# A hybrid encoder layer on one core: its last phase replanned and rearranged, with an earlier table load, one split on another engine and a third room for attention loads

## The chip, the cores and the metric

The kernel runs on one core of a Trainium2 chip. The engines of a core work side by side, each through its own queue in order, and wait for each other by semaphores: PE (TensorE) multiplies matrices, DVE (VectorE), ACT (ScalarE) and POOL (GpSimd) work on tiles, SP (SyncE) issues transfers; POOL issues some transfers as well. The metric is the device time of one execution in microseconds (us), the median of several; lower is better.

## The reference, cut to what matters

One layer is applied to 1536 tokens (a sequence of 1024 and one of 512) of width 1024, in fp32, with a feed-forward width of 2816:

```
h   = rmsnorm(x);  q, k, v, rec_x, rec_gate, g_attn, g_rec = split(h @ w_in)
A   = local_attention(rope(q), rope(k), v, sink)          # |i - j| <= 128
R   = bidir_rglru(centred_conv(rec_x)) * gelu(rec_gate)
merged = sigmoid(g_attn) * (A @ w_attn_proj) + sigmoid(g_rec) * (R @ w_rec_proj)
x   = x + rmsnorm(merged @ w_out)
h   = rmsnorm(x)
f   = (silu(h @ w_gate) * (h @ w_up)) @ w_ffn_out
y   = x + rmsnorm(f)
```

## The kernel before, in words

Tokens lie along the free axis, in three chunks of 512; 0 and 1 are the long sequence, 2 is the short one. Features lie on the 128 partitions, so a tile is 128 x 512 and a width of 1024 is eight tiles. fp32 accuracy is made out of three faster products: every operand is split into a high part (a copy by ACT into a shorter format, `hi`, or the first line of `split`) and a low part (operand less high part, on DVE or POOL, `lo`), and the products high-high, high-low and low-high are summed in PSUM (lines 353 to 355 before the last phase, 1377 to 1379 in it). A weight or operand is thus ready only when two engines have worked on it.

The start computes the first norm's factors in two halves of 256 tokens: squares by ACT, their sum over partitions by a product with ones, `Abs_reciprocal_sqrt` by ACT and three steps by DVE (`rstd_from`). ACT evaluates functions from tables, and another set of functions must first be loaded (ACT_TABLE_LOAD). Then come the projections v, k, q. `Stream` brings their weights: SP loads, ACT makes the high part, and the engine in the list `specs` the low one; entries `w_z[ZQ + j]` are the query weights. A rotary embedding of each query tile (lines 479 to 482) is done by DVE.

The middle does the RG-LRU and the attention with gate products between attention blocks. `att_load` brings a block's v, k and four q tiles through the rooms `braw`, of which there are two; a load waits until the room's last user has read it. The same SP queue carries the weight loads of `Stream` (line 318).

The last phase begins at the planner `Sched`. Each step is an `Op` on engine E (PE), V, P, A or S (SP's transfers), or Q (a transfer issued by POOL, used where it adds to what is in memory, `accum_op`), and "VP" lets it choose DVE or POOL. The planner simulates the phase with estimated times and writes each step into its engine's queue in the order in which it would start; on the chip the queues then run in that fixed order. PE's order of products is written out in a list `SEQ`: chunk 2 plainly ("B"), chunks 0 and 1 with a scheme of seven products for eight ("A"), stage by stage: attention and recurrent projections (pa, pr), out-projection (wo), FFN in (fi), FFN out (fo). Weights run through three raw rooms (`rw`) and six rooms for split ones (`sw`), gate tiles through two rooms (`ld`).

After the out-projection comes `first_norm`, for chunk 2 with 8 tiles and for chunks 0 and 1 with 16: each mix tile is loaded, multiplied by the norm's factor, and the layer's input x is added to it by a transfer that POOL issues and that accumulates into the tile (`added`). `second` squares the tile into room `a`, adds it to a sum, and stores the tile to yT. `rstd` then multiplies the sum by ones on PE (line 1195) and makes the next norm's factor; every FFN operand waits for that.

The last entries of `SEQ` are two halves of chunk 2's FFN out (`b_fo`), each 22 operand tiles (`bo`, loaded from `fsp` and split) times four PSUM banks. `b_tail` squares and copies each bank, the final `rstd` follows, and eight `last_out` multiply a tile by the factor and add it to yT by accumulating transfers.

Of the kernel before, what the change touches and what calls it, by code (L numbers as in the profile page):

```python
# [18 lines left out]
KD = 8  # L19
T = 1536  # L20
CH = 512
# [104 lines left out]
class Sched:  # L126
# [45 lines left out]
    def run(self):  # L172
        while self.programs:
# [14 lines left out]
            if eng in "SQ":  # L188
                self.t[queue] = at + (0.4 if eng == "S" else 0.7)
                self.wire = max(self.wire, at + 1.3) + op.n * 512 / 300e3  # L190
                end = self.wire + 0.7
            else:
                end = self.t[eng] = self.end(op, eng, at)
                if eng == "P":
                    self.port = end
# [8 lines left out]
def layer(ctx, tc, xT, par, w_z, w_v, w_g, w_pa, w_prA, w_prB, w_o, w_fi, w_foA, w_foB, rope, cst, yT):  # L204
# [24 lines left out]
    eps_t = const.tile([128, 1], F32, name="eps_t")  # L229
    dve.memset(eps_t, EPS)  # L230


# [137 lines left out]
    specs = [(w_v[j], wpair, dve) for j in range(2)] + [(w_z[ZK], wpair, dve), (w_z[ZK + 1], bpair, dve)]  # L370
    specs += [(w_z[ZQ + j], wpair, pool) for j in range(NQ)]
    for n in range(NL):
# [345 lines left out]
    def att_load(kv, c):  # L718
# [4 lines left out]
        def load(nm, src):  # L723
            r = b1.tile([128, 640], F32, name=f"{nm}{kv}{c}", tag="braw", bufs=2)
            n = src.shape[1] * (src.shape[2] if len(src.shape) > 2 else 1)
            sp.dma_start(r[:, :n] if len(src.shape) == 2 else r[:, :n].rearrange("p (b d) -> p b d", d=128), src)
            return r[:, :n]
# [458 lines left out]

    def rstd(a):

        done = []
        S.spawn(rstd_steps(a, done), -1)  # L1190
        yield lambda: done

    def rstd_steps(a, done):
        ps = yield from PS.take()
        yield Op("E", 4 * CH, lambda e: e.matmul(ps.t, ones, a.t, start=True, stop=True), [a], [ps])
        t = yield from HB.take()
# [25 lines left out]
    def first_norm(todo, xroom, aroom, c0, sums, queue):  # L1222

        xq, aq = [], []

        def no(x, k, n):
            yield from ()

# [8 lines left out]
        for _ in todo:  # L1237
            a, k, n = yield from get(aq)
            b = (yield from get(xq))[0]
            c, s = c0 + n, sums[n]  # L1240
            yield from tt(b.t, b.t, r[n].t, ALU.mult, [b, r[n]], [b], "VP")
            yield from added(None, xT[k * 128:(k + 1) * 128, c * CH:(c + 1) * CH], b)
            S.spawn(second(k, c, n, a, b, s, n in seen), 3)
            seen.add(n)
            queue.append(b)
# [252 lines left out]
    ROOM = [4 * i + 3 for i in range(PROD)] + [0, 1, 2, 4, 5, 6, 8, 9, 10, 12, 13, 14, 16, 17, 18, 20, 21]  # L1498
    tail, fin = {}, {}

# [7 lines left out]
    def b_fo(half):  # L1508
# [3 lines left out]
        if half == 0:  # L1512
            acc["f", 2] = yield from NM.take()
        for k in range(KF):
            s = yield from get(SQ)
# [4 lines left out]
            x.free, x.stage = True, None  # L1520
            SR.put(s)
        for i in range(4):
            m = 4 * half + i
            S.spawn(scaled("f", O_NFPOST, fof, m, 2, banks[i], True) if half == 0 else b_tail(m, banks[i]), 1)

    def b_tail(m, bank):
        o = fin[m, 2] = yield from roomy(40 + m)
        yield from square_add(("f", 2), bank, bank.t)
        yield from actv(o.t, bank.t, AF.Copy, [bank], [o], scale=P_[:, O_NFPOST + m:O_NFPOST + m + 1])
        PS.put(bank)  # L1530
# [30 lines left out]
    def build_b():  # L1561
# [14 lines left out]
        for m in range(4):  # L1576
            fin[m, 2] = yield from roomy(40 + m)
            yield from load(fin[m, 2], fof[m, 2])
        yield lambda: n_acc.get(("f", 2)) == KD
        r = acc["f", 2]  # L1580
        yield from rstd(r)
        for m in (4, 5, 6, 7, 0, 1, 2, 3):
            yield from last_out(m, 2, fin[m, 2], r)

    def start_rest():
# [101 lines left out]
```

## Time and profile before

| what | value |
|---|---|
| runs | 2469.33, 2470.05, 2472.5 us; median 2470.05 |
| profiled execution | 2475.74 us, of which the span 2474.0 |
| mean granted clock of PE | 0.991 |
| busy in the span | PE 97%, PE weight load 81%, DVE 68%, ACT 47%, POOL 31% |
| products of the last phase, lines 1377 to 1379 | the first six lines of the chain that ended last, from 17% down |

The span is the stretch that the trace covers. PE is busy nearly throughout, so an edit off PE counts only where PE waits for it, and in the serial stretch at the end.

### The profile page before, as it was taken

How to read it: one execution, taken by the hardware profiler on the slowest of the kernel's cores; microseconds unless marked ns; L12 is line 12 of the kernel's file. 1: busy time of each engine (PE TensorE's matmuls, PEld its weight loads, DVE VectorE, ACT ScalarE, POOL GpSimd, SP SyncE). 2: the span in 40 equal slices, each digit the busy share in tenths (PEclk: the TensorE clock that was granted, in tenths of full speed). 3: DMA queues.
4: the chain of work that ended last, by engine and by line, in shares of the span. 5: the costliest groups of instructions: out<-in, count | busy, mean ns of one | idle time of the engine just before them, and what ended most of it. 6: DMA issues, size and time to landing. Idle time of an engine off the chain costs nothing.

```text
span 2474.0 us, 30302 instructions
## 1 busy us (share of the span) xinstructions
PE 2409.9 (97%) x10878; PEld 1994.2 (81%) x10878; DVE 1688.5 (68%) x2454; ACT 1165.2 (47%) x1947; POOL 768.9 (31%) x602
## 2 busy tenths in 40 slices
PE   7999999999999999999999999999999999999996
PEld 5888888888878788888877888788888888888875
DVE  7864368686767665357867767875555568688794
ACT  5211567676645555444553445533333344344652
POOL 2322132424311122114334323143333333244242
PEclk9999999999999999999999999999999999999998
DMA  5222011111233332467686629422222234457557
GB/s 180 68 94 73 26 47 56 49 54 55 87 127 96 96 107 88 160 221 200 237 235 144 196 98 265 170 93 77 78 94 85 77 121 145 161 157 187 185 172 171
DMA packets 133063, 311.40 MB, mean 126 GB/s; under 512 B 14992, under 2 KB 23312, under 8 KB 132880
## 3 DMA queue, kind: packets, MB, share of 16 engines
q1 hardware_dynamic: 108880, 250.21, 30.6%
q0 software_dynamic: 22304, 57.68, 9.6%
q8 instruction: 85, 1.39, 0.2%
q10 hardware_dynamic: 1728, 1.57, 0.2%
q14 instruction: 66, 0.54, 0.1%
HBM read 215.03 MB, written 94.37 MB: 125 GB/s over the span
## 4 chain that ended last, share of the span: by engine, by line
PE 85%; issue 4%; DVE 3%; DMA 3%; POOL 2%; ACT 2%; SPq 0%; POOLq 0%; ACTq 0%; DVEq 0%
PE bk L1379 17%; PE bk L1377 17%; PE bk L1378 17%; PE pgt L354 3%; PE pgt L353 3%; PE pgt L355 3%; PE prg L354 2%; PE prx L354 2%; PE prg L355 2%; PE prx L355 2%; PE prg L353 2%; PE prx L353 2%; PE psq L355 2%; PE psq L354 2%; PE psq L353 2%
## 5 line engine op out<-in xcount | busy, mean ns | idle before, releaser
L1379 PE MATMUL bk<-ao,sw 128*128 128x512 f32 x1370 | 535.0, 390 | 2.3 <-DVE sw L964 2.3
L1377 PE MATMUL bk<-ao,sw 128*128 128x512 f32 x1370 | 536.3, 391 | 0.0
L1378 PE MATMUL bk<-ao,sw 128*128 128x512 f32 x1370 | 534.8, 390 | 0.0
L964 DVE TENSOR_TENSOR sw<-rw,sw 128x512 fp32r<-128x512 f32 (+2 forms) x358 | 313.7, 880 | 108.3 <-ACT sw L961 108.1
L964 DVE TENSOR_TENSOR co<-co,bk 128x512 f32<-128x512 f32 x326 | 218.9, 683 | 176.5 <-PE bk L1379 173.8
L961 ACT ACTIVATE sw<-rw 128x512 fp32r<-128x512 f32 (+2 forms) x381 | 228.1, 607 | 211.9 <-PE bk L1378 151.9
L1379 PEld LDWEIGHTS bk<-ao,sw 128*128 128x128 f32 x1370 | 258.1, 188 | 56.4 <-DVE sw L964 2.8
L1378 PEld LDWEIGHTS bk<-ao,sw 128*128 128x128 f32 x1370 | 258.3, 189 | 54.3 <-issue 0.8
L1377 PEld LDWEIGHTS bk<-ao,sw 128*128 128x128 f32 x1370 | 258.2, 188 | 54.2 <-issue 0.8
L1377 PE MATMUL bk<-bo,sw 128*128 128x512 f32 x656 | 258.8, 395 | 0.0
L1378 PE MATMUL bk<-bo,sw 128*128 128x512 f32 x656 | 255.9, 390 | 0.2 <-DVE bo L964 0.2
L1379 PE MATMUL bk<-bo,sw 128*128 128x512 f32 x656 | 255.8, 390 | 0.0
L961 ACT ACTIVATE sw<-tw 128x512 fp32r<-128x512 f32 (+2 forms) x138 | 81.8, 601 | 202.7 <-PE bk L1378 145.8
L304 POOL TENSOR_TENSOR w<-wr,w 128x1024 fp32r<-128x1024 f32 (+2 forms) x56 | 122.4, 2194 | 152.2 <-ACT w L303 151.8
L961 ACT ACTIVATE ao<-ta 128x512 fp32r<-128x512 f32 x166 | 101.3, 626 | 123.7 <-DVE ta L964 91.9
L353 PE MATMUL pgt<-h,w 128*128 128x512 f32 x384 | 156.4, 407 | 0.0
L354 PE MATMUL pgt<-h,w 128*128 128x512 f32 x384 | 151.4, 394 | 0.0
L355 PE MATMUL pgt<-h,w 128*128 128x512 f32 x384 | 151.2, 394 | 0.0
L622 DVE TENSOR_TENSOR i<-i,xc 128x1536 f32<-128x1536 f32 x20 | 71.1, 3589 | 113.0 <-ACT i L620 113.0
L1378 PEld LDWEIGHTS bk<-bo,sw 128*128 128x128 f32 x656 | 123.5, 188 | 27.7 <-issue 1.7
L1377 PEld LDWEIGHTS bk<-bo,sw 128*128 128x128 f32 x656 | 123.5, 188 | 27.1 <-issue 1.7
L1379 PEld LDWEIGHTS bk<-bo,sw 128*128 128x128 f32 x656 | 123.4, 188 | 25.5
(279 smaller groups left out, 4861.9 us busy)
## 6 DMA issues: line engine op xcount, KB each, us to landing
rw<-w_fi SPq DMA_DIRECT2D x88, 512.0 KB, 3.6
wr<-w_z SPq DMA_DIRECT2D x46, 512.0 KB, 3.7
ld<-gsp SPq DMA_DIRECT2D x48, 256.0 KB, 3.5
fsp<-co SPq DMA_DIRECT2D x44, 256.0 KB, 2.3
ta<-fsp SPq DMA_DIRECT2D x44, 256.0 KB, 3.9
bo<-fsp SPq DMA_DIRECT2D x44, 256.0 KB, 4.5
rw<-w_foB SPq DMA_DIRECT2D x22, 512.0 KB, 4.1
gsp<-gst POOLq DMA_DIRECT2D x42, 256.0 KB, 2.3
```

The source lines that it names most:

```text
L304: eng.tensor_tensor(out=lo, in0=x, in1=f32(hi), op=ALU.subtract)
L353: pe.matmul(ps, wh, xh, start=start and k == 0, stop=False)
L354: pe.matmul(ps, wh, xl, start=False, stop=False)
L355: pe.matmul(ps, wl, xh, start=False, stop=stop and k == n - 1)
L622: dve.tensor_tensor(out=I[d], in0=I[d], in1=xc, op=ALU.mult)
L961: yield Op("A", n, lambda e: e.activation(out, in_, func, **kw), R, W)
L964: yield Op(eng, n, lambda e: e.tensor_tensor(out=out, in0=a, in1=b, op=op), R, W)
L1377: pe.matmul(bank, wh, xh, start=first, stop=False)
L1378: pe.matmul(bank, wh, xl, start=False, stop=False)
L1379: pe.matmul(bank, wl, xh, start=False, stop=last)
```

## The change

There are eight edits in it. The planner now takes a POOL transfer to end 5.0 us after the wire is done with it, not 0.7, which reorders the queues of the last phase. ACT runs one activation of `Abs_reciprocal_sqrt` at the very start. The first query weight's low part goes to DVE. `braw` has three rooms. In `first_norm` the last three eighths of the tiles (three of chunk 2, six of chunks 0 and 1) get x by a load of SP into room `a` and an addition on DVE or POOL, in place of the accumulating transfer. In `b_fo(1)` the last four operand tiles are multiplied bank after bank, and each bank's `b_tail` starts when it is done. The eighth square is not added to the sum by DVE; a second product with ones adds it in PSUM (`rstd`'s `more`). At the end tiles 3 to 7 of yT are loaded early, and a multiplication and an addition on DVE and a plain store replace the accumulating transfer; tiles 0 to 2 keep it, and the order is 0 to 7.

```diff
@@ -188,7 +188,7 @@
             if eng in "SQ":
                 self.t[queue] = at + (0.4 if eng == "S" else 0.7)
                 self.wire = max(self.wire, at + 1.3) + op.n * 512 / 300e3
-                end = self.wire + 0.7
+                end = self.wire + (0.7 if eng == "S" else 5.0)
             else:
                 end = self.t[eng] = self.end(op, eng, at)
                 if eng == "P":
@@ -228,6 +228,7 @@
     negc, halfc = lru[:, 0, :], lru[:, 1, :]
     eps_t = const.tile([128, 1], F32, name="eps_t")
     dve.memset(eps_t, EPS)
+    act.activation(lru[:, 0, 0:1], eps_t, AF.Abs_reciprocal_sqrt)
 
 
     def rstd_from(ps, out, t, evac=None):
@@ -368,7 +369,7 @@
         return t[:, 0, :], t[:, 1, :]
 
     specs = [(w_v[j], wpair, dve) for j in range(2)] + [(w_z[ZK], wpair, dve), (w_z[ZK + 1], bpair, dve)]
-    specs += [(w_z[ZQ + j], wpair, pool) for j in range(NQ)]
+    specs += [(w_z[ZQ + j], wpair, pool if j else dve) for j in range(NQ)]
     for n in range(NL):
         specs += [(w, wpair, pool) for w in [w_z[ZRX + n]] + [w_g[i] for i in range(n - 1, n) if n] + [w_z[ZRG + n]]]
     specs += [(w_z[ZGA], wpair, pool), (w_g[NL - 1], wpair, pool)]
@@ -721,7 +722,7 @@
         nb = b_hi - b_lo
 
         def load(nm, src):
-            r = b1.tile([128, 640], F32, name=f"{nm}{kv}{c}", tag="braw", bufs=2)
+            r = b1.tile([128, 640], F32, name=f"{nm}{kv}{c}", tag="braw", bufs=3)
             n = src.shape[1] * (src.shape[2] if len(src.shape) > 2 else 1)
             sp.dma_start(r[:, :n] if len(src.shape) == 2 else r[:, :n].rearrange("p (b d) -> p b d", d=128), src)
             return r[:, :n]
@@ -1184,15 +1185,18 @@
             HB.put(sq)
         n_acc[key] += 1
 
-    def rstd(a):
+    def rstd(a, more=()):
 
         done = []
-        S.spawn(rstd_steps(a, done), -1)
+        S.spawn(rstd_steps(a, done, more), -1)
         yield lambda: done
 
-    def rstd_steps(a, done):
+    def rstd_steps(a, done, more):
         ps = yield from PS.take()
-        yield Op("E", 4 * CH, lambda e: e.matmul(ps.t, ones, a.t, start=True, stop=True), [a], [ps])
+        yield Op("E", 4 * CH, lambda e: e.matmul(ps.t, ones, a.t, start=True, stop=not more), [a], [ps])
+        for x in more:
+            yield Op("E", 4 * CH, lambda e: e.matmul(ps.t, ones, x.t, start=False, stop=x is more[-1]), [x], [ps])
+            HB.put(x)
         t = yield from HB.take()
         yield from actv(a.t, ps.t, AF.Abs_reciprocal_sqrt, [ps], [a], bias=eps_t, scale=1.0 / D)
 
@@ -1223,8 +1227,11 @@
 
         xq, aq = [], []
 
+        late = todo[len(todo) - 3 * len(todo) // 8:]
+
         def no(x, k, n):
-            yield from ()
+            if (k, n) in late:
+                yield from load(x, xT[k * 128:(k + 1) * 128, (c0 + n) * CH:(c0 + n + 1) * CH])
 
         S.spawn(from_list([(u, k, n) for u, (k, n) in zip(xroom, todo)], from_tiles(mixsp, c0), xq), 3)
         S.spawn(from_list([(u, k, n) for u, (k, n) in zip(aroom, todo)], no, aq), 3)
@@ -1239,7 +1246,10 @@
             b = (yield from get(xq))[0]
             c, s = c0 + n, sums[n]
             yield from tt(b.t, b.t, r[n].t, ALU.mult, [b, r[n]], [b], "VP")
-            yield from added(None, xT[k * 128:(k + 1) * 128, c * CH:(c + 1) * CH], b)
+            if (k, n) in late:
+                yield from tt(b.t, b.t, a.t, ALU.add, [a, b], [b], "VP")
+            else:
+                yield from added(None, xT[k * 128:(k + 1) * 128, c * CH:(c + 1) * CH], b)
             S.spawn(second(k, c, n, a, b, s, n in seen), 3)
             seen.add(n)
             queue.append(b)
@@ -1496,7 +1506,7 @@
 
 
     ROOM = [4 * i + 3 for i in range(PROD)] + [0, 1, 2, 4, 5, 6, 8, 9, 10, 12, 13, 14, 16, 17, 18, 20, 21]
-    tail, fin = {}, {}
+    tail, fin, last_sq = {}, {}, []
 
     def roomy(i):
         if i // 2 not in tail:
@@ -1511,7 +1521,8 @@
             banks.append((yield from PS.take()))
         if half == 0:
             acc["f", 2] = yield from NM.take()
-        for k in range(KF):
+        late = 4 * half
+        for k in range(KF - late):
             s = yield from get(SQ)
             x = B[(KF * half + k) % 6]
             yield lambda: x.stage == "fo"
@@ -1519,13 +1530,28 @@
                 yield from mm_op(banks[i], s, 128 * i, x, k == 0, k == KF - 1)
             x.free, x.stage = True, None
             SR.put(s)
+        if half == 0:
+            for i in range(4):
+                S.spawn(scaled("f", O_NFPOST, fof, i, 2, banks[i], True), 1)
+            return
+        ss = []
+        for k in range(KF - late, KF):
+            ss.append((yield from get(SQ)))
+            x = B[(KF + k) % 6]
+            yield lambda: x.stage == "fo"
         for i in range(4):
-            m = 4 * half + i
-            S.spawn(scaled("f", O_NFPOST, fof, m, 2, banks[i], True) if half == 0 else b_tail(m, banks[i]), 1)
+            for k in range(KF - late, KF):
+                yield from mm_op(banks[i], ss[k - KF + late], 128 * i, B[(KF + k) % 6], False, k == KF - 1)
+            S.spawn(b_tail(4 + i, banks[i]), 1)
 
     def b_tail(m, bank):
         o = fin[m, 2] = yield from roomy(40 + m)
-        yield from square_add(("f", 2), bank, bank.t)
+        if m < KD - 1:
+            yield from square_add(("f", 2), bank, bank.t)
+        else:
+            last_sq.append((yield from HB.take()))
+            yield from actv(last_sq[0].t, bank.t, AF.Square, [bank], [last_sq[0]])
+            n_acc["f", 2] += 1
         yield from actv(o.t, bank.t, AF.Copy, [bank], [o], scale=P_[:, O_NFPOST + m:O_NFPOST + m + 1])
         PS.put(bank)
 
@@ -1576,11 +1602,20 @@
         for m in range(4):
             fin[m, 2] = yield from roomy(40 + m)
             yield from load(fin[m, 2], fof[m, 2])
+        xs = {}
+        for m in range(3, KD):
+            xs[m] = yield from roomy(29 + m)
+            yield from load(xs[m], yT[m * 128:(m + 1) * 128, 2 * CH:3 * CH])
         yield lambda: n_acc.get(("f", 2)) == KD
         r = acc["f", 2]
-        yield from rstd(r)
-        for m in (4, 5, 6, 7, 0, 1, 2, 3):
+        yield from rstd(r, last_sq)
+        for m in range(3):
             yield from last_out(m, 2, fin[m, 2], r)
+        for m in range(3, KD):
+            o, x = fin[m, 2], xs[m]
+            yield from tt(o.t, o.t, r.t, ALU.mult, [o, r], [o])
+            yield from tt(x.t, x.t, o.t, ALU.add, [o, x], [x])
+            yield from store(yT[m * 128:(m + 1) * 128, 2 * CH:3 * CH], x)
 
     def start_rest():
```

Line numbers after the second edit are higher by one, and by more further down. The order of the queues changes at many places; three of them follow.

DVE, in the q projection: the rotary steps of two query tiles (lines 479 to 482, in the changed kernel 480 to 483), of before, then of the changed kernel. `w_997<-wr_224,w_997` is the low part of the first query weight.

```order
L481 TENSOR_TENSOR qst<-qst,rope_t 32x512
L482 TENSOR_TENSOR qst<-qst,qsw 32x512
L479 STREAM_SHUFFLE qsw<-qst 32x512
L480 TENSOR_TENSOR qsw<-qsw,rope_t 32x512
L481 TENSOR_TENSOR qst<-qst,rope_t 32x512
```

```order
L482 TENSOR_TENSOR qst<-qst,rope_t 32x512
L483 TENSOR_TENSOR qst<-qst,qsw 32x512
L305 TENSOR_TENSOR w_997<-wr_224,w_997 128x1024
L480 STREAM_SHUFFLE qsw<-qst 32x512
L481 TENSOR_TENSOR qsw<-qsw,rope_t 32x512
```

The low part stands between the last step of one tile and the first of the next.

ACT, in the projections of chunks 0 and 1: gate tiles `ld` (loaded, then passed through the sigmoid), splits of weights (`sw` from `rw` or `tw`), a copy out of PSUM (`co`) and the split of an operand (`ao`), of before, then of the changed kernel.

```order
L961 ACTIVATE ld_8222<-ld_8222 128x512
L961 ACTIVATE ld_8223<-ld_8223 128x512
L961 ACTIVATE ld_8222<-ld_8222 128x512
L961 ACTIVATE sw_8427<-rw_8432 128x256 x2
L961 ACTIVATE ao_1_8198<-ta_8226 128x512
L961 ACTIVATE co_8219<-bk_8240 128x512
L961 ACTIVATE sw_8428<-tw_8234 128x256
L961 ACTIVATE sw_8428<-rw_8432 128x256
L961 ACTIVATE ao_1_8206<-ta_8226 128x512
```

```order
L962 ACTIVATE ld_8223<-ld_8223 128x512
L962 ACTIVATE ld_8224<-ld_8224 128x512
L962 ACTIVATE sw_8428<-rw_8433 128x256 x2
L962 ACTIVATE sw_8429<-tw_8235 128x256
L962 ACTIVATE co_8220<-bk_8236 128x512
L962 ACTIVATE sw_8429<-rw_8433 128x256
L962 ACTIVATE sw_8430<-rw_8431 128x512
L962 ACTIVATE ld_8223<-ld_8223 128x512
L962 ACTIVATE ao_1_8199<-ta_8227 128x512
```

The third gate tile of these stood right behind the second; now five splits of weights and a copy stand between them.

POOL, in the norm of chunks 0 and 1: the multiplication of a mix tile (`ao` by `nm`), the accumulating transfers of x (`ao<-xT`, `ta<-xT`) and additions to the sums of squares (`nm`, `ta`), of before, then of the changed kernel.

```order
L958 DMA ao_2_11561<-xT 128x512 x2
L964 TENSOR_TENSOR nm_8232<-nm_8232,ao_2_11535 128x512
L958 DMA ao_2_11568<-xT 128x512 x2
L958 DMA ao_2_11574<-xT 128x512
L964 TENSOR_TENSOR ta_8226<-ta_8226,ao_2_11557 128x512
L958 DMA ao_2_11574<-xT 128x512
L964 TENSOR_TENSOR nm_8232<-nm_8232,ao_2_11582 128x512
L958 DMA ta_8227<-xT 128x512
L958 DMA ao_2_11683<-xT 128x512 x2
L964 TENSOR_TENSOR ta_8226<-ta_8226,ao_2_11600 128x512
L958 DMA ta_8224<-xT 128x512
```

```order
L959 DMA ao_2_11565<-xT 128x512 x2
L959 DMA ao_2_11572<-xT 128x512 x2
L965 TENSOR_TENSOR ao_2_11578<-ao_2_11578,nm_8232 128x512
L965 TENSOR_TENSOR ta_8228<-ta_8228,nm_8232 128x512
L965 TENSOR_TENSOR ao_2_11702<-ao_2_11702,nm_8231 128x512 x2
L965 TENSOR_TENSOR ao_2_11702<-ao_2_11702,ao_2_11658 128x512
L965 TENSOR_TENSOR ta_8227<-ta_8227,ao_2_11625 128x512
L965 TENSOR_TENSOR ta_8227<-ta_8227,ao_2_11648 128x512
L965 TENSOR_TENSOR nm_8233<-nm_8233,ao_2_11625 128x512
```

The transfers end with the tenth, and multiplications and additions of the later tiles stand in their place. PE's order differs in 19 lines: the product that asks for chunk 2's sum stands 6 products later, the two that ask for those of chunks 0 and 1 stand 34 and 35 earlier, one product with ones is new at the end, and the last 48 products go bank after bank.

## Rows read from the trace of the kernel before

**Rows 1.** The page: busy us of each engine, share of the span, instructions.

```profile
PE 2409.9 (97%) x10878; PEld 1994.2 (81%) x10878; DVE 1688.5 (68%) x2454; ACT 1165.2 (47%) x1947; POOL 768.9 (31%) x602
```

**Rows 2.** Timeline of PE: start, us, operation, [idle before <-what ended it].

```profile
100.06 0.50 PE L355 MATMUL psq<-h,w 128*128 128x512 f32 x1 [1.83 <-POOL w L304]
...
707.32 0.36 PE L353 MATMUL pss<-kh,qh 128*128 128x256 f32 x1 [3.82 <-DVE sm L776]
...
851.06 0.41 PE L353 MATMUL pss<-kh,qh 128*128 128x384 f32 x1 [1.98 <-DVE sm L776]
...
1289.39 2.07 PE L1195 MATMUL bk<-nm,ones 128*128 128x512 f32 x2 [5.54 <-DVE nm L964]
...
1359.46 0.50 PE L1379 MATMUL bk<-ao,sw 128*128 128x512 f32 x1 [2.34 <-DVE sw L964]
...
1554.72 1.92 PE L1195 MATMUL bk<-nm,ones 128*128 128x512 f32 x2 [3.00 <-DVE nm L964]
```

**Rows 3.** Stretches: us, busy of PE, PEld, DVE, ACT, POOL, PEclk, DMA share, GB/s.

```profile
2447.40:2450.12 2.72, 2.72 (x12) 1.90 (x11) 1.27 (x2) 1.93 (x4) 0.00 (x0) 1.00 0.00 0
100.06:106.06 6.00, 6.00 (x19) 4.79 (x20) 5.81 (x7) 0.00 (x0) 2.83 (x2) 0.72 0.57 190
...
1289.39:1297.39 8.00, 8.00 (x21) 5.69 (x22) 4.92 (x7) 5.43 (x8) 2.93 (x4) 0.62 0.67 192
...
1554.72:1562.72 8.00, 8.00 (x24) 5.48 (x25) 3.99 (x7) 3.71 (x6) 0.00 (x0) 0.79 0.95 376
```

**Rows 4.** Timelines of ACT and of DVE at the start.

```profile
10.43 1.28 ACT L235 ACT_TABLE_LOAD   x1
...
10.45 1.23 DVE L304 TENSOR_TENSOR w<-wr,w 128x1024 fp32r<-128x1024 f32 x1 [1.28 <-ACT w L303]
12.23 0.42 DVE L238 SCALAR_TENSOR_TENSOR nt0a<-pst0a,rstd0a 128x256 f32<-128x256 f32 x1 [0.56 <-ACT rstd0a L235]
```

**Rows 5.** Timeline of DVE in the q projection.

```profile
96.11 0.68 DVE L482 TENSOR_TENSOR qst<-qst,qsw 32x512 f32<-32x512 f32 x1
```

**Rows 6.** Timeline of SP ahead of the two attention waits.

```profile
699.88 0.33 SPq L318 DMA_DIRECT2D wr<-w_z  x1
700.56 0.32 SPq L726 DMA_DIRECT2D qr<-qsp  x1
...
842.93 0.33 SPq L318 DMA_DIRECT2D wr<-w_z  x1
845.18 0.32 SPq L726 DMA_DIRECT2D qr<-qsp  x1
```

**Rows 7.** Timeline of ACT in chunk 2's norm.

```profile
1281.00 0.63 ACT L961 ACTIVATE bo<-bo 128x512 f32<-128x512 f32 x1 [1.42 <-DMA bo<-xT]
```

**Rows 8.** Timeline of ACT in the projections of chunks 0 and 1.

```profile
1343.71 0.63 ACT L961 ACTIVATE ld<-ld 128x512 f32<-128x512 f32 x1 [8.63 <-DMA ld<-gsp]
```

**Rows 9.** DMA queues in 1510 to 1556: packets, MB, share of 16 engines.

```profile
q0 software_dynamic: 2304, 4.20, 51.1%
q1 hardware_dynamic: 3574, 8.03, 50.2%
```

**Rows 10.** Timeline of ACT in the norm of chunks 0 and 1.

```profile
1540.09 0.63 ACT L961 ACTIVATE ao<-ao 128x512 f32<-128x512 f32 x1 [1.37 <-DMA ao<-xT]
```

**Rows 11.** The end: timelines; DMA of 2466 to 2474 in 40 slices; page, issue to landing.

```profile
2441.92 0.69 DVE L964 TENSOR_TENSOR bo<-bo,bo 128x512 fp32r<-128x512 f32 x1
...
2452.61 2.07 PE L1195 MATMUL bk<-nm,ones 128*128 128x512 f32 x2 [2.49 <-DVE nm L964]
...
2457.61 4.91 DVE L964 TENSOR_TENSOR ao<-ao,nm 128x512 f32<-128x512 f32 x8
...
2458.60 7.09 POOL L1558 DMA_DIRECT2D yT<-ao  x8 [27.44 <-DVE ao L964]
...
DMA  9998999999999999999999999966300000000000
...
fsp<-co SPq DMA_DIRECT2D x44, 256.0 KB, 2.3
```

## The prediction

> **What bounds the kernel now.** I began with the busy times on the profile's page: TensorE works for 97% of the span [rows 1], 2409.9 of 2474.0 us, so about 64 us of its idle time is all that an edit of this kind can win, besides the clock. Then came the timeline of TensorE, whose brackets give the idle time ahead of an instruction and what ended it. Six waits of 2 to 5.5 us stand in places that the diff touches [rows 2]: for the low part of the first query weight (1.83), for the scores of two attention blocks (3.82 and 1.98), for the squares of the two residual norms (5.54 and 3.00), and for one low part of a split weight (2.34). At the end of the program comes a serial tail. Last I asked what each wait costs beyond itself. In a stretch without waits TensorE has the full clock and 12 products take 2.72 us, 0.227 each [rows 3]. In the 6 us after the query weight's wait the granted clock is 0.72, in the 8 us after the norms' waits 0.62 and 0.79 [rows 3]. So each short wait costs its own length and a lost share of the clock: 6 x 0.28 = 1.68 us (the row at 100.06 stands for four that read 0.72), 8 x 0.38 = 3.04 at 1289, and 8 x 0.21 = 1.68 at 1554.
>
> **The sum, part by part.**
>
> *Table at the start.* Now the table for the first norm is loaded between the first weight's split and its norm, 1.28 us on ACT at 10.43 [rows 4]. With the new first activation it is loaded before any data arrive, and Square and Copy need no other set (in the trace they run on either side of that load with none of their own). TensorE does not get all of it: VectorE has the weight's low part to make first, until 10.45 + 1.23 = 11.68, and its first norm step now starts at 12.23 [rows 4]. So 0.55 at most comes through there; bounds 0.3 and the whole 1.28. I take **0.5**, since VectorE's row is the nearer one. The Trainium skill, page "ScalarE: Activation LUTs", section "What ACT_TABLE_LOAD costs", prices a switch at 2.66 us, the load and a drain of 1.38; the row has a load of 1.28, and the norm step that needs the activation behind it starts 0.52 after the load's end, which leaves no room for that drain. By the page alone this term would read 2.66.
>
> *First query weight.* Its low part goes from POOL to VectorE. There it stands behind the last step of a rotary embedding, which starts at 96.11 and takes 0.68 [rows 5], so 96.8 + 1.23 (the same operation in rows 4) = 98.0. TensorE, which became idle at 100.06 - 1.83 = 98.23 [rows 2], need not wait. Gain 1.83 + 1.68 = **3.5**; the bound below is 1.5, if VectorE comes 2 us late to it. Behind it VectorE does another rotary step 1.2 us later, which ends in a transfer that attention reads only hundreds of us on.
>
> *Three rooms for attention loads.* The loads run in SP's order. Before the second attention wait the fourth query load was issued at 845.18, though the weight load ahead of it left at 842.93 + 0.33 [rows 6]: 845.18 - 843.26 = 1.9 us of waiting for one of the two rooms. A third takes that off, and the wait of 1.98 all but goes: 1.87 + 1.68 = 3.55. Before the first wait the load (700.56) stands right behind a weight load (699.88 + 0.33) [rows 6], so SP's own order holds it and a room buys 0.3. Together **3.85**; from 2 (some other operand is late next) to 9 (both waits go wholly, 3.82 + 1.68 more).
>
> *Residual norm of chunk 2.* Now eight accumulating transfers, issued by POOL, add x to the tiles. The fifth of them was squared at 1281.00 [rows 7], the sum was asked for at 1289.39 - 5.54 = 1283.85 [rows 2]. Three of the eight are now ordinary loads that SP issues ahead of time, and an addition each on VectorE or POOL. So the sum can be ready some 3 to 4.5 us after 1281.0 (a square 0.63 from that row, and an addition of 0.69 as in rows 11, for the items then left), 1284 to 1285.5, and the matmul that asks for it stands six rows later, 1283.85 + 6 x 0.227 = 1285.2. The wait and its clock, 5.54 + 3.04 = 8.6, nearly go: **8.0**; 5 if the additions queue behind other work.
>
> *Split weight at 1357.* ACT had stood 8.63 us, until 1343.71, for a gate load [rows 8] whose room was held by a slow accumulating transfer, and made up its backlog of splits until TensorE ran out of one. In the new order six splits and copies stand ahead of that load. I take the whole 2.34 + 1.68 = **4.0**; nothing, if another instruction of ACT stands so.
>
> *Residual norm of chunks 0 and 1.* In 1510 to 1556 the 16 accumulating transfers moved 4.20 MB and took 51.1% of the engines' time; ordinary ones moved 8.03 MB in 50.2% [rows 9]. So an accumulated byte cost about two others, and the stretch is full. Six of the sixteen become loads and POOL issues ten. The tenth was squared at 1540.09 [rows 10]. With two sums and the last additions behind it I expect both between 1542 and 1546. But the sum is now asked for 34 rows earlier, at 1551.7 - 34 x 0.227 = 1544. Of 3.0 + 1.68 = 4.7 I take **3**; nothing, if the sum slips as far as its matmuls moved.
>
> *Tail.* Now TensorE ends its last product at 2450.12, waits 2.49 and does the sum in 2.07, 2452.61 to 2454.68; the norm's steps follow until the multiplications start at 2457.61 (eight in 4.91, 0.61 each), and POOL's eight accumulating transfers, issued in 7.09 from 2458.60, move data until 29 slices of 0.2 us after 2466 [rows 11], 2471.8, 2.2 before the end. New: a bank's last twelve products stand together, so the last operand, ready at 2441.92 + 0.69 [rows 11], is wanted some 1.1 us before that: products end at 2451.2. The seven squares are summed by then, one matmul on them covers the last square, the second follows: 2 us, 2453.2. The steps (2.93) give 2456.1; three multiplications 1.8, and five pairs of multiplication and addition 5 x 1.3 = 6.5, give 2464.4. The last plain store lands 2.3 later as other stores do [rows 11], 2466.7, and 1.8 to 2.2 of closing give 2468.5 to 2469. Gain **5.5**; 4.4 if the last pairs stretch, 7.2 if the last operand is no wait.
>
> *New waits.* The planner's table reorders VectorE, ACT, POOL and SP in the whole last phase. I cannot cost it row by row; the three waits listed there make 10.9 us, so others of that kind may arise; I put **-2**, from 0 to -10.
>
> Sum: 0.5 + 3.5 + 3.85 + 8 + 4 + 3 + 5.5 - 2 = 26.4 us. The profiled execution took 2475.74 (its span 2474.0 and 1.74 around it), so its like would take 2449.3; it lay 5.7 above the median of the runs, 2470.05, and the median becomes **2443.7**.
>
> **Rivals.**
>
> *The transfers stay late.* If the loads land no sooner than accumulations did, since all share engines that are 95% busy after 1554 [rows 3], the norm of chunks 0 and 1 is waited for as before and the wait at 1357 returns; chunk 2's norm keeps half: 3 + 4 + 4 less, 11 of the 26, so 2454.7. Rows 9 speak against it (each moved byte costs half), the full stretch for it. The Trainium skill, page "DMA: Bandwidth & Descriptors", section "Issuing engines are not separate DMA queues", says that another issuing engine saves only the sequencer's time to issue; by that the moves from POOL to SP are worth nothing in the queue, as in this rival; the trace agrees that both share the engines, and not that a byte costs the same in both.
>
> *Both attention waits go, and no new wait comes.* 5.2 + 2 more: 2436.5.
>
> *Slower.* The six x loads stand on SP ahead of weight loads of the FFN and need rooms that the last output projection frees. If SP stands there, weights come late and TensorE starves. It has split weights for six slots of twelve products, 6 x 2.72 = 16 us, and as much in raw ones behind them, so it loses only what SP stands beyond some 32 us; to undo the sum and 5 us more that must be a stand of over 60, for 2475 or more. The longest such stand in the rows, ACT's 8.63 for a load, cost 2.34. I give it little.
>
> *No change.* The waits move instead of going, as a planner's estimates may do: then the last term is -25 and the time within 5 us of 2470 (0.2%, about what a measurement of this kernel can tell from no change).
>
> **How the numbers follow.** Forecast, 2435 to 2452: 0.62. Transfers late, 2452 to 2462: 0.17. Better than 2435, or the attention rival at its edge: 0.09. No change: 0.07. Slower: 0.05. Faster by over 0.2% (under 2465) holds the first three and a little from between, 0.88; same 0.07, slower 0.05. The range of 8 in 10 runs from the forecast's lower edge to where the late transfers end: 2435 to 2460, leaving out 0.09 below and some 0.13 above.
>
> **What would show it.** No ACT table load near 10; no TensorE wait at the first query weight and a granted clock of 1 behind it; the second attention wait gone and the first still near 3.5; the chunk-2 norm's wait under 1 us; ACT's longest stand near 1340 under 3; the norm of chunks 0 and 1 with a wait under 1.5; the multiplications at the end starting near 2456 less what was won before, and 12.5 us from there to the end. Wrong would make it: a new TensorE wait of over 3 us in the last phase, above all where FFN weights start; or the norms' sums ending as late as before, with the loads landing after the accumulations.

## The result, and the profile after

The changed kernel took 2460.92 us, median of five runs (2459.42 to 2461.39), the kernel before beside it 2470.05 (2469.33 to 2475.83): ratio 0.995, interval 0.9938 to 0.9962. It is faster, by 9 us where 26 were forecast, and 0.9 us above the range. On later occasions the kernel before ran at medians of 2476.0 to 2477.2, and a second comparison gave 2462.57 against 2476.53, ratio 0.9945 (0.9932 to 0.9957), 14 us. The two profiles first shown lie 16.3 us apart in their spans, and the accounts below are of these two.

The page of the changed kernel, its span, busy times and the two DMA queues that matter:

```profile
span 2457.7 us, 30313 instructions
PE 2405.4 (98%) x10880; PEld 1990.5 (81%) x10880; DVE 1699.3 (69%) x2458; ACT 1167.6 (48%) x1949; POOL 774.4 (32%) x597
...
q1 hardware_dynamic: 111616, 255.19, 31.6%
q0 software_dynamic: 20288, 54.01, 8.8%
```

The timeline of TensorE at the places of [rows 2]:

```profile
702.10 0.55 PE L354 MATMUL pss<-kh,qh 128*128 128x256 f32 x1 [3.54 <-DVE sm L777]
...
845.35 0.41 PE L354 MATMUL pss<-kh,qh 128*128 128x384 f32 x1 [0.44 <-DVE sm L777]
...
1281.44 2.07 PE L1196 MATMUL bk<-nm,ones 128*128 128x512 f32 x2 [3.49 <-DVE nm L965]
...
1536.51 2.08 PE L1196 MATMUL bk<-nm,ones 128*128 128x512 f32 x2 [7.15 <-POOL nm L965]
```

The waits at the query weight and at the split weight have no row any more; the first attention wait is as it was, the second fell to 0.44. Chunk 2's norm is still waited for, 3.49 us, and the norm of chunks 0 and 1 for 7.15 in place of 3.00. The stretches behind them (columns as in [rows 3]):

```profile
96.00:102.00 6.00, 6.00 (x28) 4.84 (x27) 5.78 (x9) 1.97 (x4) 3.39 (x3) 1.00 0.67 218
702.10:708.10 6.00, 6.00 (x18) 4.99 (x19) 3.56 (x17) 2.91 (x10) 0.06 (x1) 0.52 0.12 46
...
1281.44:1289.44 8.00, 8.00 (x27) 5.84 (x28) 5.09 (x7) 5.05 (x8) 2.65 (x2) 0.79 0.41 109
1536.51:1544.51 8.00, 8.00 (x23) 5.46 (x24) 4.84 (x6) 2.48 (x4) 1.67 (x1) 0.74 0.51 166
```

The full clock stays through the q projection. What holds the norms is on VectorE and POOL. First chunk 2, then chunks 0 and 1, each VectorE and then POOL:

```profile
1264.40 4.69 DVE L965 TENSOR_TENSOR rw<-rw 128x256 f32<-128x256 f32 x1
1264.63 2.92 POOL L965 TENSOR_TENSOR bo<-bo,nm 128x512 f32<-128x512 f32 x2
1267.12 1.68 POOL L965 TENSOR_TENSOR tb<-tb,nm 128x512 f32<-128x512 f32 x1
...
1510.68 6.28 DVE L965 TENSOR_TENSOR ao<-ao,ao 128x512 f32<-128x512 f32 x1
1516.89 1.78 DVE L965 TENSOR_TENSOR sw<-rw,sw 128x512 fp32r<-128x512 f32 x1
...
1510.91 1.76 POOL L965 TENSOR_TENSOR ao<-ao,nm 128x512 f32<-128x512 f32 x1
1512.17 1.75 POOL L965 TENSOR_TENSOR ta<-ta,nm 128x512 f32<-128x512 f32 x1
1513.41 3.00 POOL L965 TENSOR_TENSOR ao<-ao,nm 128x512 f32<-128x512 f32 x2
1516.49 1.64 POOL L965 TENSOR_TENSOR ao<-ao,ao 128x512 f32<-128x512 f32 x1
```

A VectorE operation that takes 0.42 us elsewhere takes 4.69 while POOL multiplies three tiles, and one of 0.69 takes 6.28 while it multiplies four. ACT shows who waits for that:

```profile
1514.13 0.61 ACT L962 ACTIVATE ao<-ao 128x512 f32<-128x512 f32 x1
1517.00 0.63 ACT L962 ACTIVATE ao<-ao 128x512 f32<-128x512 f32 x1 [2.26 <-DVE ao L965]
1519.31 0.63 ACT L962 ACTIVATE ao<-ao 128x512 f32<-128x512 f32 x1 [1.67 <-DVE ao L965]
```

The squares of chunks 0 and 1 waited for transfers in [rows 10]; now they wait for VectorE's additions. In the 27 us in which these squares are summed VectorE was busy for 20.36 in the kernel before and is for 26.72 in the changed one, held time counted as busy; first before, then after:

```profile
1525.00:1552.00 27.00, 26.73 (x118) 21.80 (x117) 20.36 (x28) 12.85 (x23) 13.11 (x13) 1.00 1.09 278
```

```profile
1510.00:1537.00 27.00, 19.85 (x87) 16.19 (x86) 26.72 (x25) 14.68 (x26) 17.97 (x13) 0.94 1.03 298
```

The end, timelines of TensorE, VectorE, POOL and SP, answering to [rows 11]:

```profile
2439.42 0.40 PE L1389 MATMUL bk<-bo,sw 128*128 128x512 f32 x1
2439.66 1.02 PE L1196 MATMUL bk<-nm,ones 128*128 128x512 f32 x2
2440.51 1.12 PE L1198 MATMUL bk<-hb,ones 128*128 128x512 f32 x2
...
2444.57 2.50 DVE L965 TENSOR_TENSOR ao<-ao,nm 128x512 f32<-128x512 f32 x4
...
2452.41 0.69 DVE L965 TENSOR_TENSOR ao<-ao,ao 128x512 f32<-128x512 f32 x1
...
2445.70 2.66 POOL L1584 DMA_DIRECT2D yT<-ao  x3 [26.86 <-DVE ao L965]
...
2447.82 5.65 SPq L951 DMA_DIRECT2D yT<-ao  x5
```

The sum follows the last product with no wait; from the last product's end to the end of the span are 2457.7 - 2439.8 = 17.8 us, before 2474.0 - 2450.1 = 23.9.

### The profile page after: what moved, and what is told of

Its sections match the earlier page's. It is cut to its first block, busy times and chain, and to the rows that moved or that the text cites. A ratio compares the mean times of both kernels' runs of the same rounds, so it can differ in the third digit from the quotient of the medians.

```text
span 2457.7 us, 30313 instructions
## 1 busy us (share of the span) xinstructions
PE 2405.4 (98%) x10880; PEld 1990.5 (81%) x10880; DVE 1699.3 (69%) x2458; ACT 1167.6 (48%) x1949; POOL 774.4 (32%) x597
## 5 line engine op out<-in xcount | busy, mean ns | idle before, releaser
L1387 PEld LDWEIGHTS bk<-bo,sw 128*128 128x128 f32 x656 | 123.6, 188 | 27.7 <-issue 1.7
```

The lines of the kernel that those rows point to most:

```text
L1387: pe.matmul(bank, wh, xh, start=first, stop=False)
```

## The experiments

In all of them "asked for" means the place of the matmul with ones in TensorE's order, and "complete" is the end of the last addition to a sum, counted from the norm's first matmul with ones (in chunks 0 and 1: to the first of the two sums). Ratios are to the kernel before, run beside each. The runs are of four later occasions, each on another chip, so the medians of different occasions are compared with care. How far two medians of one kernel can lie apart is shown by the kernel before against itself: 0.9989 (0.9978 to 1.0000), 3 us.

| run | median us | ratio, interval | wait chunk 2 | wait chunks 0, 1 | sums complete |
|---|---|---|---|---|---|
| before (two profiles) | 2470 to 2477 | | 5.54, 7.38 | 3.00, 3.00 | 31.0 and 33.0; 47.0 |
| before, again | 2473.99 | 0.9989, 0.9978 to 1.0000 | 7.38 | 3.00 | 33.0; 47.0 |
| changed, again | 2462.57 | 0.9945, 0.9932 to 0.9957 | 3.49 | 7.16 | 30.3; 43.7 |
| late tiles on VectorE | 2453.92 | 0.9909, 0.9896 to 0.9921 | 0.92 | 4.52 | 27.7; 41.7 |
| asked later | 2450.77 | 0.9894, 0.9881 to 0.9908 | 3.49 | none | 30.3; 43.8 |
| both | 2447.84 | 0.9886, 0.9873 to 0.9900 | 1.44 | none | 28.3; 41.8 |
| no late tiles | 2456.10 | 0.9915, 0.9902 to 0.9927 | 3.98 | 2.06 | 29.4; 48.8 |
| norms on VectorE | 2449.07 | 0.9890, 0.9875 to 0.9905 | 0.92 | 1.23 | 27.7; 47.3 |
| late in chunk 2 alone | 2452.55 | 0.9906, 0.9889 to 0.9923 | 0.92 | none | 27.7; 49.7 |
| old planner cost | 2471.52 | 0.9977, 0.9967 to 0.9988 | 5.44 | 7.79 | 28.9; 43.0 |
| front edits alone | 2471.25 | 0.9975, 0.9965 to 0.9986 | 5.63 | 4.15 | 31.1; 48.2 |
| planner cost alone | 2465.20 | 0.9962, 0.9949 to 0.9974 | 5.59 | 2.75 | 31.0; 49.5 |
| end edits alone | 2471.61 | 0.9986, 0.9976 to 0.9996 | 5.59 | 3.22 | 31.1; 47.2 |

**The kernel before again.**

> The kernel before, unchanged, for a second profile. Its first profiled execution took 2475.74 us, 5.7 above the median of the runs then shown. Theory: one of the waits on which the sum was built is not there in an ordinary execution, so this profile is near 2470 and lacks 4 to 6 us of TensorE's waits or of granted clock (first suspects: the 2.34 us at 1357 and the gate load on which ACT stood 8.63 us). Rival: the waits are the same within 1 us in every execution and the 5.7 us are spread over small differences of the clock; then the profile is near 2470 with the same six waits, and the sum was wrong for other reasons alone.

The profile took 2476.34 with the same six waits, in part longer:

```profile
99.74 0.50 PE L355 MATMUL psq<-h,w 128*128 128x512 f32 x1 [1.84 <-POOL w L304]
705.13 0.55 PE L353 MATMUL pss<-kh,qh 128*128 128x256 f32 x1 [3.53 <-DVE sm L776]
1360.97 0.50 PE L1379 MATMUL bk<-ao,sw 128*128 128x512 f32 x1 [3.48 <-DVE sw L964]
```

The stretches behind the first two:

```profile
99.74:105.74 6.00, 6.00 (x26) 4.95 (x27) 5.81 (x7) 0.60 (x1) 2.86 (x2) 1.00 0.59 186
705.13:711.13 6.00, 6.00 (x19) 4.97 (x20) 3.53 (x17) 2.90 (x10) 0.06 (x1) 0.56 0.13 46
```

So the theory of a missing wait fell, and the first profile was no outlier: of 25 runs on that occasion 19 lay at 2472 to 2478. The rival fell too: the profile is not near 2470, and its waits differ from the first by up to 1.84 us (7.38 for 5.54 at chunk 2's norm). What differs is what the clock takes: behind the same 1.84 us at the query weight it did not fall at all here (1.00, against 0.72 in [rows 3]), and behind the attention wait it fell further (0.56).

**The changed kernel again.** (No edit.)

> The changed kernel, unchanged, once more. The first comparison gave 2460.92 against 2470.05 (9 us), but the kernel before then ran at 2477.0 on another occasion (15 runs, 2472.1 to 2483.5), and its two profiles took 2475.74 and 2476.34. Theory: the kernel before is the one that varies, and the changed kernel stays at 2460 to 2462, so that beside a before of 2474 to 2477 the gain reads 14 to 16 us, as the two profiles show (16.3). Rival: the occasion shifts both alike; then the changed kernel takes 2465 to 2468 and the gain stays at 9.

2462.57 beside 2476.53: mostly the kernel before shifted, by 6.5 us, the changed one by 1.7. Of the 17 us by which the gain fell short of 26, 5 lie in that first median.

**Late tiles on VectorE alone.**

```diff
-            yield from tt(b.t, b.t, r[n].t, ALU.mult, [b, r[n]], [b], "VP")
+            yield from tt(b.t, b.t, r[n].t, ALU.mult, [b, r[n]], [b], "V" if (k, n) in late else "VP")
...
-                yield from tt(b.t, b.t, a.t, ALU.add, [a, b], [b], "VP")
+                yield from tt(b.t, b.t, a.t, ALU.add, [a, b], [b])
```

> The changed kernel, but the late tiles of both norms are multiplied and added to on VectorE alone, never on POOL; the matmuls that ask for the sums stay within 3 rows of where they were. Theory: POOL's multiplications one after another (4.1 us in chunk 2's norm, 7.3 in that of chunks 0 and 1) hold VectorE's next operation for as long (4.69 and 6.28 us instead of 0.42 and 0.69), and with it the additions and sums. Then no VectorE operation there is over 2.5 us, the waits of 3.49 and 7.15 fall to under 1 and to 1 to 3, and with the clock 7 to 10 us go: 2451 to 2454. Rival: the sums are late because of the squares and transfers; then the waits stay within 1 us and the time at 2460 to 2462.

The long operation is gone from the same place, and both sums are complete sooner, by 2.6 and 2.0 us:

```profile
1507.75 0.69 DVE L965 TENSOR_TENSOR ao<-ao,ao 128x512 f32<-128x512 f32 x1
1508.59 0.69 DVE L965 TENSOR_TENSOR sw<-rw,sw 128x512 fp32r<-128x512 f32 x1
...
1514.04 1.78 DVE L965 TENSOR_TENSOR ao<-ao,nm 128x512 f32<-128x512 f32 x1
1515.74 1.77 DVE L965 TENSOR_TENSOR sw<-rw,sw 128x512 fp32r<-128x512 f32 x1
...
1511.89 3.38 POOL L965 TENSOR_TENSOR ta<-ta,ao 128x512 f32<-128x512 f32 x2 [3.44 <-ACT ao L962]
1515.22 5.15 POOL L965 TENSOR_TENSOR nm<-nm,ao 128x512 f32<-128x512 f32 x3
...
1531.62 1.22 PE L1196 MATMUL bk<-nm,ones 128*128 128x512 f32 x1 [4.52 <-POOL nm L965]
```

Right for chunk 2 (0.92). In chunks 0 and 1 4.52 remain, above the 1 to 3 expected: the long hold was part of it. Shorter ones stay: while POOL makes these five additions to the sums, five operations of VectorE in a row take 1.77 to 1.79 where 0.69 is usual.

**Asked later.**

```diff
+            if c0 == 0 and s is sums[0]:
+                s.w = (s.w[0] + 8.0, s.w[1])
             yield from rstd(s)
```

> The changed kernel, but the planner takes the first sum of chunks 0 and 1 to be ready 8 us later, so that the matmul that asks for it stands 36 rows (8.2 us of products) later, where it stood in the kernel before. Theory: the wait of 7.15 us is there because the matmul was moved up further (34 rows, 7.7 us) than the sum was hastened; then it goes nearly wholly and 7 to 9 us with the clock: 2452 to 2454. Rival: the first operands of the FFN behind it are then late by the same, and TensorE waits for those: 2459 to 2462.

The sum is complete when it was (43.8), TensorE comes to it at 44.6 and does not wait, nor at an FFN operand behind it; 2450.77, a little more than expected of it. So the 7.15 us were there because the matmul was moved up 7.7 us and the sum by 3.3.

**No late tiles.** `late = []`.

> The changed kernel, but no tile of the two norms is late: all 24 get x by the accumulating transfer, as before. The planner's cost of these transfers stays at 5.0 us, so chunk 2's sum is asked for where it was in the kernel before and that of chunks 0 and 1 twelve rows later than there. Theory (the late tiles brought little as they are): chunk 2's wait is again near 5.5, the other falls from 7.15 to under 1, and the time is 2455 to 2459. Rival (the late tiles brought all that the norms gained): the waits are 5 to 6 and 3 or more, and the time is 2463 or more.

As the theory had it in time, though not in the waits (3.98 and 2.06). As they were built, the late tiles cost 5 to 9 us: the kernel without them is at 2456.10 and 0.9915, with them at 2460.92 and 0.9950 or 2462.57 and 0.9945. That is mostly the early request: without them the planner asks for the sum of chunks 0 and 1 some 45 products later, and from the first profile of the changed kernel to this one TensorE gains 5.5 us at that norm and loses 0.4 at chunk 2's.

**Both repairs.** The two diffs above together.

> The changed kernel with both repairs: the late tiles of the two norms on VectorE alone, and the sum of chunks 0 and 1 asked for 8 us of the planner's time later. Theory: what each took away goes together, so the waits of the norms are 0.9 in chunk 2 (as in the run with the late tiles on VectorE) and 0 in chunks 0 and 1 (as in the run that asks later), and the time is 3 to 4 us under the 2450.8 of the run that asks later: 2446 to 2449. Rival: VectorE is then too full for the first FFN operands, which are late next: 2450 or more.

2447.84, the lowest median, 15 us under the changed kernel (the interval of the next run overlaps with this one's). Chunk 2's wait is 1.44, and one of 1.14 for a split is new at 1366.

**All of the norms on VectorE.** "VP" becomes VectorE in the multiplications, additions and sums of the norms.

> The changed kernel with all multiplications, additions and sums of the two norms on VectorE; POOL keeps only their transfers. The planner then asks for chunk 2's sum where the changed kernel does and for that of chunks 0 and 1 42 rows (9.5 us) later. What counts here is how long after the first product with ones of the norm the sum is complete: before 31.0 and 47.0 us, changed 30.3 and 43.7, with the late tiles on VectorE 27.7 and 41.7. Theory: VectorE and POOL, adding to one sum in turn and holding each other, are what keeps it; then the second falls to 38 to 40, TensorE waits for neither norm by more than 1.5, and the time is 2447 to 2450. Rival: VectorE alone has too much to do (its additions, sums and splits of weights); then the sum is complete no sooner than 41.7, splits come late, and the time is 2450 or more.

The time is as the theory had it, its reason is not: the sum of chunks 0 and 1 is complete at 47.3, no sooner than with POOL's help, and the wait there is short (1.23) because the matmul asks 42 products later. With the arithmetic on POOL gone no VectorE operation of that norm is held, 0.69 each. But the squares wait for the accumulating transfers again, 4.7 us in five waits, and VectorE for what stands behind them in ACT's queue:

```profile
1522.34 0.63 ACT L962 ACTIVATE ao<-ao 128x512 f32<-128x512 f32 x1 [1.84 <-DMA ao<-xT]
1523.52 0.69 DVE L965 TENSOR_TENSOR sw<-rw,sw 128x512 fp32r<-128x512 f32 x1 [3.87 <-ACT sw L962]
```

**Late tiles in chunk 2 alone.** `late = todo[5:] if c0 else []`, with the late tiles on VectorE and the sum asked for 4 us later.

> Late tiles in chunk 2's norm alone, on VectorE; all sixteen tiles of chunks 0 and 1 get x by the accumulating transfer, and their first sum is taken to be ready 4 us later, so that it is asked for 63 rows (14.3 us) later than in the changed kernel. Theory: for chunks 0 and 1 only the place of the product that asks counts, and the sum, complete 48.8 us after the norm's first product without late tiles, is there in time; no wait at that norm, 0.9 to 1.5 in chunk 2, and 2446 to 2450, as the run with both repairs (2447.8). Rival: the first FFN operands are then late by what the sum is, or ten accumulating transfers fewer also helped the weights; then waits of 2 us or more behind the norm and 2452 or more.

The rival came true. No wait at the norm, but one behind it, at an FFN operand, with the clock at 0.91 over the 20 us around it:

```profile
1606.56 0.50 PE L1389 MATMUL bk<-ao,sw 128*128 128x512 f32 x1 [2.04 <-ACT ao L962]
```

So in chunks 0 and 1 the late tiles are worth something too once the sum is not asked for ahead of time: 4.7 us between this run and the one with both repairs. The medians are of two occasions, but the two profiles agree: TensorE passes the same work within 1 us up to 1600 and loses 4.9 us by 1700. The runs differ also in the place of the request, 27 products later here, since the sum without late tiles is complete 8 us later.

**The old planner cost.** 5.0 becomes 0.7 in the changed kernel.

> The changed kernel with the planner's old cost of a POOL transfer (0.7 for 5.0). ACT's third gate tile stands right behind the second again, and the sums are asked for 15 rows (3.4 us, chunk 2) and 6 rows (1.4 us) earlier than in the changed kernel. Theory: the order of ACT's queue makes the wait near 1357, so it comes back with 2 to 3.5 us, and the norms' waits grow to 6 to 7 and 8 to 9: 2470 to 2474. Rival: with fewer accumulating transfers the gate load is no longer late whatever the order; then no wait there, and 2463 to 2468.

```profile
1353.17 0.79 PE L1389 MATMUL bk<-ao,sw 128*128 128x512 f32 x1 [3.06 <-DVE sw L965]
...
1337.35 0.63 ACT L962 ACTIVATE ld<-ld 128x512 f32<-128x512 f32 x1 [8.74 <-DMA ld<-gsp]
```

ACT's stand of [rows 8] is back within 0.1 us of its length, and with it TensorE's wait; the time is as expected, 9 us over the changed kernel. The norms' waits, 5.44 and 7.79, are a little under the 6 to 7 and 8 to 9 expected.

**The planner cost alone,** in the kernel before.

> The kernel before with the planner's cost of a POOL transfer alone changed (5.0 for 0.7). The sum of chunks 0 and 1 is asked for 12 rows (2.7 us) later, that of chunk 2 where it was. Theory: the order of ACT's queue around 1340 is what made the wait at 1357, so this wait goes (2.3 to 3.5 us and 1.7 of clock), the wait at 1553 falls from 3.0 to 1 or 2, and the time is 5 to 8 us under before. Rival: the wait at 1357 needs the late tiles too, whose transfers no longer hold the queue; then 0 to 2 us under before.

No wait near 1357, though ACT still stands 6.69 us for a gate load there: the splits that TensorE needs now go ahead of the next one. 0.9962, 9 us, more than the 5 to 8 expected; the late tiles are not needed for it. In the profiles 4.3 of the 7.9 us come at the split weight. The wait of chunks 0 and 1 stayed near its size, since the sum came later too (49.5).

**The front edits alone** (table, query weight, three rooms).

> The kernel before with three edits alone: the table loaded first, the first query weight's low part on VectorE, three rooms for attention loads. By the profile of the changed kernel these give 1.4, 3.5 and 2.3 us, together 7.2 under before; the prediction had 0.5, 3.5 and 3.85, together 7.85. Rival: the waits of the last phase grow by what was won ahead of them, since its transfers run by their own time; then 0 to 4.

0.9975, 6.2 us (5.3 between the medians), nearer to the theory. But the rival came as well: TensorE reached chunk 2's norm 6.1 us sooner than in the first profile of before, then the waits at the split weight (3.15 for 2.34) and of chunks 0 and 1 (4.15 for 3.00) grew, and at the end 1.2 us were left. That profile is the slowest of the eight runs, so its loss may be more than the usual one.

**The end edits alone.**

> The kernel before with the edits at its end alone: the last four operand tiles bank after bank, the last square summed on TensorE, five of eight tiles by a load and an addition. In the profile of the changed kernel the stretch from the last product to the end is 18.05 us, 23.88 before. Theory: 5.8 us come off wherever the rest stands: 2470 to 2472 beside a before of 2476.5. Rival: the five early loads delay the last operands or the end was bounded by something else; then 3 or less.

0.9986 (0.9976 to 0.9996), 1 to 6 us: the median falls by 4.4, the expectation is at its edge. By the medians alone this can't be told from the kernel before against itself (0.9989). In the profile 17.3 us lie between the last product and the end, 6.5 less than before, so the gain is there; 1.4 of it are lost ahead of the last product, where the prediction had 1.1.

## Why the prediction missed

By its own terms, from how far ahead the changed kernel's profile is at the same product:

| term | forecast | measured | where it is read |
|---|---|---|---|
| table at the start | 0.5 | 0.5 | VectorE idle ahead of its first norm step for 0.55, now 0.05 |
| (first weight's arrival) | | 0.9 | its split starts at 9.36, now 8.48 |
| first query weight | 3.5 | 3.5 | 4.9 ahead at the first attention wait |
| three rooms | 3.85 | 2.3 | 7.25 ahead behind the second |
| chunk 2's norm | 8.0 | 3.4 | 10.6 ahead behind it |
| split weight at 1357 | 4.0 | 4.3 | 14.9 ahead behind it |
| norm of chunks 0 and 1 | 3 | -4.5 | 10.4 ahead behind it |
| tail | 5.5 | 5.6, and 0.3 at 2382 | 10.7 ahead at 2430, 16.3 at the end |
| new waits | -2 | 0 | none found |
| sum | 26.4 | 16.3 | spans 16.3 apart |

**The step that failed** is "With two sums and the last additions behind it I expect both between 1542 and 1546", and its like in chunk 2, "So the sum can be ready some 3 to 4.5 us after 1281.0". Counted from each norm's first matmul with ones these say 34 to 38 us and 26 to 27; complete were the sums at 43.7 and 30.3. I had taken the transfers as the only thing that the sums wait for, since the profile showed ACT waiting for them [rows 7, 10], and had priced a moved addition at 0.69 on whichever engine. The transfers did become few enough: in chunks 0 and 1 ACT no longer waits for them, in chunk 2 for 1.9 us in place of 11.2. But the additions moved off them went to VectorE and POOL, and the new plan lets POOL do multiplications that VectorE did before (three of chunk 2 and five of chunks 0 and 1, for none and one), where POOL's operations hold VectorE's. The trace of before had a row that should have warned, a rotary step that takes 0.68 elsewhere, while POOL works on the query weight:

```profile
98.53 4.36 DVE L480 TENSOR_TENSOR qsw<-qsw,rope_t 32x512 f32<-32x512 f32 x1
```

The runs with the late tiles on VectorE show the long holds as the cause of most of the 3.49 (0.92 without them) and of 2 to 3 of the 7.15. They are not the whole excess. No run completed the sums as forecast: at best at 27.7 and 41.7, with POOL's shorter holds still there, and with the norms' arithmetic on VectorE alone at 27.7 and 47.3, with the squares of chunks 0 and 1 waiting for transfers again. How the rest in chunks 0 and 1 divides between the engines and the transfers stays open.

The larger part of the second wait is the other half of the same step. I wrote that the sum "is now asked for 34 rows earlier" and took it to be ready by then; the planner had, too: for a hold by POOL it charges a VectorE operation at most its own length once more. The run that asks later shows it: the same sum, no wait.

"The transfers stay late" came nearest among the rivals in size (2454.7) for a wrong reason: its waits at the norms came, that at 1357 did not. That a moved transfer gains nothing in itself is not what the runs show: in the changed kernel the squares of chunks 0 and 1 wait for no transfer, and the late tiles there are worth 4.7 us where nothing asks too early.

The terms of the split weight and the tail were right in mechanism and size, and each is shown by a run of its own. That of the query weight was right in mechanism; its size holds for the first profile of before, where 1.7 of the 3.5 us are the clock behind the wait, and would have been 1.8 in the second, where the clock did not fall. The table's term was right, by the row that it was taken from: VectorE's idle time there is 0.55 to 0.57 us in the four profiles with the old order and 0.05 or none in the ten with the new. The first product starts 1.4 us sooner since the first weight also arrived sooner, which varies (split at 8.96 to 9.79 in the four, at 8.11 to 9.15 in the ten); whether an edit has to do with that stays open.

The three rooms gave 2.3 for 3.85: the clock behind the first attention wait, which stayed as predicted, read 0.52 where it had been 0.72, 1.2 us, and 0.44 of the second wait remained. Of the 3.4 us at chunk 2's norm 2.05 are the shorter wait and the rest is the clock, 0.79 for 0.62 over 8 us; behind the same wait of 3.49 it read 0.65 and 0.62 in two other runs, so that part is luck.

## What to carry to other kernels

Where a transfer is replaced by arithmetic, count the arithmetic on the engine that then makes the sum, and look for the longest operations on VectorE while POOL works: their excess over the usual is the price. A hastened result gains only if the matmul that asks for it does not move up by more; read completion and request as two times from one common event. And profile the kernel before twice, and compare on the same occasion, before a sum of small waits is set against one median.

## What was not expected of the hardware

One VectorE operation with two inputs in SBUF was held through three or four POOL operations in a row (4.69 us against 0.42, 6.28 against 0.69), not through one. The Trainium skill, page "SBUF — State Buffer", section "Who interferes with whom", says that such an instruction contends with a POOL instruction that reads SBUF and that the loser waits for the whole of the other's; the trace agrees that it waits, and shows it waiting through several. It is not always so: in the run with the late tiles on VectorE POOL made additions just as close together, two and three to one sum, and VectorE got one operation in for each, at 1.8 us. What makes the difference no run here shows.

The clock behind a wait is no constant of the wait: after 1.83 us it fell to a mean of 0.72 over 6 us in one execution and not at all in the next, after the same 3.49 us to 0.79, 0.65 and 0.62 over 8 us, and behind the first attention wait (3.5 to 4.1 us) it read 0.50 to 0.75 in the fourteen profiles. Six such waits can so move an execution by several us, by an estimate from these rows. The runs of the kernel before agree with it: the slowest, 2486.49, has a mean granted clock of 0.988, the fastest, 2467.48, 0.994.
